# One fp32 decoder layer on a single core: the order of weight sums, of q's low parts, of a norm's steps and of attention's value products

## The chip, the cores and the metric

The kernel runs on one core of one Trainium2 chip. A core has a matrix engine (TensorE, in the profile PE, with its weight load as PEld), three engines for elementwise work (VectorE, DVE; ScalarE, ACT; GpSimd, POOL) and a queue engine (SyncE, SP) that here only issues transfers. SP, ACT and POOL issue transfers between DRAM and the core's own memory (SBUF); all of them take their instructions in order. The metric is the time of one execution on the device in microseconds (us).

## The reference

The layer takes x (512 tokens x 1024) and multiplies it with one weight matrix of 1024 x 9216. The columns are split into nine groups of 1024. Cut to what matters:

```python
h = x @ w_in
ua, va, za, qh, kh, vh, zb, ga, gb = split(h)
ua = gelu(ua)
va = layer_norm(gelu(va), a_ln_g, a_ln_b)
sa = einsum("gts,bnsgc->bntgc", tril(w_s), va in 4 chunks x 8 groups) + a_b_s
ya = ua * sa * silu(za)
q = rope(qh) * 64 ** -0.5            # 8 heads, two maps of 64 each
k = rope(kh)
o = diff_attention(q, k, vh, lam)    # softmax 1 - lam * softmax 2, causal, times v
yb = rms_norm(o) * g * silu(zb)
m = sigmoid(ga) * (ya @ w_branch_a) + sigmoid(gb) * (yb @ w_branch_b)
out = layer_norm(alpha * x + m @ w_out + sigmoid(x @ w_pg) * (p @ w_ple))
```

## The kernel before

Every fp32 product is made of three matmuls of the faster fp32r type: each operand is cut into a high part and a low part (for a weight: ACT copies `wh`, line 334; DVE subtracts to `wl`, line 337), and high x high, low x high and high x low are added in PSUM. One such matmul, 128x128 by 128x512, is called a product here.

PE works through stages one after another: k, q (pair 0), zb (pair 0), v, attention with the groups of k, q and zb of the next pair of heads between its small matmuls, ua, za, va, ga, gb, pg, the per-layer embedding, the two branch projections wb and wa, and the output. v, va, ga, gb, pg, wb and wa use a Strassen-like scheme, `quad`: seven steps of 24 products in place of eight, on quarters of the 1024x1024 weight and sums of them. In line with that, a weight quad has 14 half quarters or sums to be split.

There are two ways to those sums of weights. In a `quad` plan, POOL adds the next quarter onto the one in SBUF with an accumulating transfer (`follow`, line 308), as soon as DVE has read the old one for its low part; tiles that hold sums are called `wa`, others `wr`, three buffers each. In a `ready_quad` plan (before: only wb), four sums of two halves each lie in DRAM (`wsd`); they are made there during attention by `make_sums`: SP copies a quarter (a "begin", line 281), later POOL adds another onto it (an "add", line 279), and SP loads them afterwards like any weight (line 301).

The order of all this is written out by hand. `later(n, fn)` puts a step behind the n-th product from now, and tables of such numbers set where each step is issued: `TURN_Q` and the stack numbers for q's rotary step of pair 0 (multiplications on DVE, a join on POOL at lines 660 and 661, high halves `hl` on ACT at 666, low halves on POOL at 671, then the stacks: SP copies `q<-hl`, line 687), `ROPE` for later pairs, `VALUES` for the products of attention weights with v (line 771; `at` is their copy from the transposes, line 762), `TAIL` for a head's norm behind its values, `NORM` for va's layer norm (mean and factor on DVE and POOL, centring at line 1069, shift at 1073, statistics at 1065), `MAKE` for the sums in DRAM, `SPLITS` for a quad's `wh` and `wl`. On ACT the quads' intermediate sums `s` are copied from PSUM (line 563). For v, DVE and ACT also cut sums of x into parts, `piece` (line 865).

Of the kernel before, what the change touches and what calls it, by code (L numbers as in the profile page):

```python
# [39 lines left out]
HIGH = (2,)  # L40
LOW = (12,)
ROPE = (2, 6, 8, 14, 18)
STACK = (14, 4)
FIRST_STACK = (20, 4)
SWAP = 132
# [2 lines left out]
PERIOD = (13, 16, 20, 23)  # L48
COMBINE = (10, 10, 13, 11)
TURN = (23, 24, 32, 27)  # L50
VALUES = (34, 36, 41, 41)
TAIL = (2, 14, 26, 44)
NORM = (4, 50, 148, 172)
SPLITS = {"wb": ((4, 7), (13, 16)), "": ((1, 4), (8, 12))}
BEHIND = (8, 14)
GELU = 22
SILU = (20,)
SPATIAL = (222, 22)
MAKE = (2, 26, 146, 170, 290, 314, 440, 490)
TABLES = (30, 44)  # L60
TURN_K = (16, 19, 22, 25, 29, 36, 40)
TURN_Q = (28, 31, 36, 40, 46, 84, 88)
LAMBDAS = (130, 250, 324, 332)
FIRST_GATE = 168
SUMS_OF_X = (60, 66, 84, 90, 150, 158, 174, 182)
SUMS_OF_Y = (90, 120, 150, 180, 250, 268, 286, 304)
XS = (2, 2, 50, 14)
EARLY = 0
HELD = 2
CUT_YB = (2, 6)  # L70
# [30 lines left out]
def token_units(off):  # L101
    return [("t", off + c * T, kk) for c in range(2) for kk in range(4)]
# [16 lines left out]
def plan():  # L119

    units, steps, made_of = [], [], {}

    def add(name, w, us):
        for u in us:
            steps.append((name, len(units), "", None))  # L130
            units.append((w, u))

    def quad(name, w, us):
        first, last = len(units), {}
        units.extend((w, u) for u in us)
        for chain, quarter in CHAINS:
            for j in range(2):
                steps.append((name, first + QUARTERS[quarter][j], chain, last.get((chain, j))))
                last[chain, j] = len(steps) - 1

    def ready_quad(name, w, us):
        first = len(units)
        units.extend((w, u) for u in us)
        for what in READY:
            for j in range(2):
                unit = ("sum", what, j) if isinstance(what, int) else first + QUARTERS[what][j]
                steps.append((name, unit, "xy"[j], None))
        for q, us in QUARTERS.items():
            made_of[q] = [first + u for u in us]

    cols = [c for _, u in rope_units(KO, 0) + rope_units(QO, 0) for c in u]
    add("kq", "in", [("c", cols, kk) for kk in range(4)])
    add("zb", "in", feature_units(ZB, 2))
    add("ua", "in", feature_units(UA, EARLY))
    quad("v", "in", token_units(VO))
    for p in range(1, 4):
        add("k", "in", rope_units(KO, p))
        add("q", "in", rope_units(QO, p))
        add("zb", "in", feature_units(ZB + 2 * p * P, 2))
    add("ua", "in", feature_units(UA + EARLY * P, KT - EARLY))  # L160
    add("za", "in", feature_units(ZA, 8))
    quad("va", "in", token_units(VA))
    quad("ga", "in", token_units(GA))
    quad("gb", "in", token_units(GB))
    quad("pg", "pg", token_units(0))
    add("ple", "ple", [("p", 1), ("p", 0)])
    ready_quad("wb", "b", token_units(0))
    add("wa", "a", token_units(0))
    add("out", "out", token_units(0))
    return units, steps, made_of  # L170
# [33 lines left out]
def hybrid_layer(ctx: ExitStack, tc: tile.TileContext, a, out: bass.AP):  # L204
# [61 lines left out]


    sums = []
    wsd = dram.tile([4, 2, P, 1024], F32, name="wsd")

    def weights(unit):
        return W[unit] if isinstance(unit, int) else wsd[unit[1], unit[2]]

    def make_sums(at):

        def step(n, what, of, j):
            source = weights(("sum", of, j) if isinstance(of, int) else MADE_OF[of][j])
            if what == "add":
                pool.dma_start(out=wsd[n, j], in_=source, accum_op=OP.add, max_dma_last_dim=4096)
            else:  # L280
                sp.dma_start(out=wsd[n, j], in_=source)

        for i, (n, what, of) in enumerate(MAKING):
            for j in range(2):
                later(at[i] + 12 * j, step, n, what, of, j)

    def load(u, pieces=1, first=sp):
        if u >= len(STEPS) or u in raw or STEPS[u][3] is not None:
# [65 lines left out]
    def next_pair(name, i):  # L354
        u = cursor[0]
        assert STEPS[u][0] == name, (STEPS[u][0], name)
        cursor[0] += 2
        for j in range(4):
            assert u + j in raw, (u, j)
        run(prep(u))  # L360
        run(prep(u + 1))

        def ask(at, v, fits=lambda chain: True):
            if v < len(STEPS) and fits(STEPS[v][2]):
                later(at, lambda: run(load(v)))


        for v in range(u + 4, u + 8):
            ask(1, v, lambda chain: chain in ("x", "y"))
        within = [bool(v < len(STEPS) and STEPS[v][2]) for v in range(u, u + 6)]  # L370
        ask(1 if within[2] else 20, u + 6)
        ask(9, u + 5, lambda chain: chain != "b" and chain != "c")
        ask(12, u + 7, lambda chain: chain != "a" and (chain or within[4]))
        for j, at in enumerate(SPLITS.get(name, SPLITS[""])):

            spread(u + 2 + j, *(BEHIND if i == 5 and j and name != "wb" else at))
        return split.pop(u), split.pop(u + 1)

    def run(gen):
# [269 lines left out]

    def rope(name, p, banks=None, at=None, stack=STACK):  # L650

        A, B = banks or (pp(), pp())
        m, parts = [], []

        def turn(bank, table):
            m.append(ap_.tile([P, T], F32, name="m", tag="m", bufs=6))
            dve.tensor_tensor(out=m[-1], in0=bank, in1=table, op=OP.mult)

        def join():
            pool.tensor_tensor(out=m[0], in0=m[0], in1=m[3], op=OP.subtract)  # L660
            pool.tensor_tensor(out=m[2], in0=m[2], in1=m[1], op=OP.add)

        def high():
            parts.append(ap_.tile([P, 4, T], F32R, name="hl", tag="hl"))
            for j in range(2):
                act.activation(parts[0][:, j, :], m[2 * j], AF.Copy)

        def low():
            hl = parts[0]
            for j in range(2):  # L670
                pool.tensor_tensor(out=hl[:, 3 - j, :], in0=m[2 * j], in1=hl[:, j, :].bitcast(F32),
                                   op=OP.subtract)
            for hd in range(2):
                later(stack[0] + stack[1] * hd, get, hd)

        def get(hd):


            h = 2 * p + hd
            for n in ("k", "kx") if name == "k" and p else (name,):  # L680
                s = ap_.tile([P, 2, T], F32R, name=n, tag=n, bufs=3)
                stacks[n, h] = s
                for i in range(2):
                    rows = parts[0][2 * hd + i:P:4]
                    if n == "kx":
                        rows = rows[:, ::-1]
                    sp.dma_start(out=s[:, i, :].bitcast(F32), in_=rows.bitcast(F32))
            if name == "k" and p == 0:
                later(SWAP + 6 * hd, change_over, h)

        def change_over(h):
            s = ap_.tile([P, 2, T], F32R, name="kx", tag="kx", bufs=3)
            stacks["kx", h] = s
            for b in range(4):
                sp.dma_start(out=s[b:P:4].bitcast(F32), in_=stacks["k", h][3 - b:P:4].bitcast(F32))

        at = at or ROPE[:2] + ROPE
        for i, bank in enumerate((A, B)):
            if not banks:
                feature_group(bank, name, xh, xl)  # L700
            later(at[2 * i], turn, bank, cs)
            later(at[2 * i + 1], turn, bank, sn)
        for n, fn in zip(at[4:], (join, high, low)):
            later(n, fn)
# [186 lines left out]
            s = slice((k % 2) * T + i * P, (k % 2) * T + (i + 1) * P)  # L891
            three(bank, h[:, s], l[:, s], xh[:, k, :], xl[:, k, :], k == 0, k == KT - 1)
    rope("k", 0, first_kq[:2], TURN_K, FIRST_STACK)
    rope("q", 0, first_kq[2:], TURN_Q, FIRST_STACK)
    gate_b(0, (pbank("tr", 1), pbank("po", 1)), FIRST_GATE)

    ua = big.tile([P, KT, T], F32, name="ua", tag="U")
# [31 lines left out]
    quad("v", operands(xh, xl, [of_piece(j) for j in range(4)]),  # L929
         ([pp(), pp()], [pbank("sc", 2) for _ in range(2)], [pp(), pbank("tx", 1)]), place_v, v_done)  # L930
    sums.clear()
    make_sums(MAKE)
    for p in range(1, 4):
        attention(p - 1, BEGIN)
        rope("k", p)
# [125 lines left out]
    def va_norm(t):  # L1061
        st = small([P, 2, 6], "vst", 4)
        z = va[:, t, :]
        for c in range(2):
            dve.bn_stats(out=st[:, c, :], in_=va[:, t, c * T:(c + 1) * T])
        mv, rs = rstd_of(st)

        def centre():
            dve.scalar_tensor_tensor(out=z, in0=z, scalar=mv[:, 0:1], in1=ga_t,
                                     op0=OP.subtract, op1=OP.mult)  # L1070

        def shift():
            dve.scalar_tensor_tensor(out=z, in0=z, scalar=rs[:, 0:1], in1=ba_t,
                                     op0=OP.mult, op1=OP.add)

        later(8, centre)
        later(16, shift)

    def spatial(g):
        sa = pbank("tr" if g % 2 else "po", 1)  # L1080
# [233 lines left out]
```

## Time and profile before

| | us |
|---|---|
| three runs | 630.01, 630.9, 635.1 |
| their median | 630.9 |
| the profiled execution | 631.16 |
| its span on the core | 629.5 |
| PE's first product (k and q) | 5.27 |
| zb | 27.96 |
| v | 38.84 |
| attention | 79.95 |
| ua | 215.2 |
| za | 274.7 |
| va | 318.70 |
| ga | 358.40 |
| gb | 396.51 |
| pg | 441.4 |
| per-layer embedding | 481.3 |
| wb | 492.15 |
| wa | 530.2 |
| output | 575.6 |

The profile is of one execution, taken by the hardware; the rows of stages are the start of their first product. An engine's share of the span is the time in which an instruction of it ran. A row of the timeline has the start, the duration, the engine, the line, the operation with its output and inputs, the count of instructions in the row, and in brackets how long the engine was idle before it and what ended that. The granted clock is that of PE as a share of full speed.

### The profile page before, as it was taken

What the parts mean: (1) busy time and instruction counts of PE and PEld (TensorE: products, weight loads), DVE (VectorE), ACT (ScalarE), POOL (GpSimd) and SP (SyncE); (2) the same over time, 40 slices, a digit from 0 to 9 for tenths busy, and PEclk for the clock granted to TensorE, in tenths of its full rate; (3) what the DMA queues carried; (4) which work ended last, traced back from release to release, by engine and by line L of the source; (5) the groups of instructions that cost most, each with busy time, mean ns of one, the idle gap of its engine ahead of it and who ended that gap; (6) DMA issues with size and microseconds to landing.
All of it is one profiled execution on the core that took longest, in us unless ns stands there. A gap on an engine that the chain in (4) does not pass through costs nothing.

```text
span 629.5 us, 8313 instructions
## 1 busy us (share of the span) xinstructions
PE 615.2 (98%) x2929; PEld 509.7 (81%) x2929; DVE 452.1 (72%) x767; ACT 314.4 (50%) x510; POOL 131.2 (21%) x132
## 2 busy tenths in 40 slices
PE   8999999999999999999999999999999999999994
PEld 5887788888888888888887888788888888888884
DVE  5898667878878866844874796868757758676386
ACT  5544575554654655565464765445556446232200
POOL 2174003714424320220012131321120000000011
PEclk9999999999999999999999999999999999999998
DMA  8678895575555525436869779898997954865102
GB/s 301 205 201 203 222 325 203 157 179 199 202 134 201 204 74 141 154 131 218 281 176 254 190 192 215 247 206 247 244 215 275 399 185 155 287 209 185 34 35 100
DMA packets 45210, 125.66 MB, mean 200 GB/s; under 512 B 5744, under 2 KB 6576, under 8 KB 45040
## 3 DMA queue, kind: packets, MB, share of 16 engines
q1 hardware_dynamic: 35232, 95.04, 42.7%
q0 software_dynamic: 7200, 25.50, 21.7%
q10 hardware_dynamic: 2736, 4.59, 1.9%
q8 instruction: 23, 0.38, 0.2%
q14 instruction: 19, 0.16, 0.1%
HBM read 101.91 MB, written 19.01 MB: 192 GB/s over the span
## 4 chain that ended last, share of the span: by engine, by line
PE 69%; DMA 13%; issue 6%; DVE 6%; ACT 4%; POOL 2%; SPq 0%; ACTq 0%; DVEq 0%; POOLq 0%
PE ps_pp L238 39%; PE ps_sc L238 11%; DMA wa<-in_w 7%; PE ps_tx L238 5%; PE ps_sc L726 3%; DMA wr<-in_w 3%; PE ps_po L771 3%; DVE wl L337 3%; PE ps_tr L238 2%; PE ps_po L238 2%; ACT wh L334 2%; DMA xt<-in_xT 2%; PE ps_tr L760 1%; DMA xr<-in_xT 1%; PE ps_tr L1082 1%
## 5 line engine op out<-in xcount | busy, mean ns | idle before, releaser
L337 DVE TENSOR_TENSOR wl<-wr,wh 128x1024 fp32r<-128x1024 f32 x90 | 115.0, 1283 | 37.7 <-ACT wh L334 37.5
L334 ACT ACTIVATE wh<-wr 128x1024 fp32r<-128x1024 f32 x90 | 94.0, 1053 | 73.5 <-DMA wr<-in_w 28.5
L238 PE MATMUL ps_pp<-xh,wh 128*128 128x512 f32 x296 | 119.3, 403 | 0.6 <-ACT wh L264 0.6
L238 PE MATMUL ps_pp<-xh,wl 128*128 128x512 f32 x296 | 117.1, 396 | 0.1
L238 PE MATMUL ps_pp<-xl,wh 128*128 128x512 f32 x296 | 117.1, 396 | 0.0
L337 DVE TENSOR_TENSOR wl<-wa,wh 128x1024 fp32r<-128x1024 f32 x46 | 55.7, 1222 | 29.4 <-ACT wh L334 29.3
L238 PEld LDWEIGHTS ps_pp<-xh,wl 128*128 128x128 f32 x296 | 55.7, 188 | 11.3 <-DVE wl L265 0.4
L238 PEld LDWEIGHTS ps_pp<-xh,wh 128*128 128x128 f32 x296 | 55.8, 188 | 10.5 <-ACT wh L264 1.1
L238 PEld LDWEIGHTS ps_pp<-xl,wh 128*128 128x128 f32 x296 | 55.7, 188 | 10.3 <-DVE xl L265 0.2
L739 ACT ACTIVATE p<-p,sth 128x128 f32<-128x128 f32 (+3 forms) x64 | 35.5, 556 | 50.5 <-DVE sth L737 50.4
L334 ACT ACTIVATE wh<-wa 128x1024 fp32r<-128x1024 f32 x46 | 48.0, 1054 | 22.5 <-DMA wa<-in_w 16.9
L308 POOL DMA_DIRECT2D wa<-in_w x30 | 26.1, 869 | 129.6 <-DVE wl L337 93.5
L1055 POOL TENSOR_TENSOR rs<-mv,mhalf 128x1 f32<-128x1 f32 x8 | 10.5, 1312 | 174.2 <-DVE mv L1053 174.2
L733 DVE CUSTOM_DVE_ANT_0 p<-ps_sc,mask 128x128 f32<-128x128 f32 (+3 forms) x64 | 31.0, 484 | 11.8 <-PE ps_sc L726 11.7
L238 PE MATMUL ps_pp<-wl,xh 128*128 128x512 f32 x80 | 31.3, 391 | 1.0 <-DVE wl L337 1.0
L238 PE MATMUL ps_pp<-wh,xh 128*128 128x512 f32 x80 | 31.2, 390 | 0.0
L238 PE MATMUL ps_sc<-wl,xsh 128*128 128x512 f32 x80 | 31.2, 390 | 0.0
L238 PE MATMUL ps_sc<-wh,xsh 128*128 128x512 f32 x80 | 31.2, 390 | 0.0
L238 PE MATMUL ps_pp<-wh,xl 128*128 128x512 f32 x80 | 31.2, 390 | 0.0
L238 PE MATMUL ps_sc<-wh,xsl 128*128 128x512 f32 x80 | 31.1, 389 | 0.0
L797 POOL TENSOR_TENSOR f<-ss,mhalf 128x4 f32<-128x4 f32 x8 | 9.0, 1123 | 81.8 <-DVE ss L796 60.0
L771 PEld LDWEIGHTS ps_po<-v,at 128*128 128x128 f32 x160 | 22.5, 190 | 3.7 <-ACT at L762 1.3
(340 smaller groups left out, 1371.4 us busy)
## 6 DMA issues: line engine op xcount, KB each, us to landing
wr<-in_w SPq DMA_DIRECT2D x78, 512.0 KB, 4.2
wa<-in_w POOLq DMA_DIRECT2D x30, 512.0 KB, 7.9
wa<-in_w SPq DMA_DIRECT2D x13, 512.0 KB, 4.7
wr<-in_w POOLq DMA_DIRECT2D x10, 512.0 KB, 8.6
k<-hl SPq DMA_DIRECT2D x16, 256.0 KB, 2.5
q<-hl SPq DMA_DIRECT2D x16, 256.0 KB, 2.5
wsd<-in_w POOLq DMA_DIRECT2D x8, 512.0 KB, 7.7
kx<-hl SPq DMA_DIRECT2D x12, 256.0 KB, 2.6
```

The costliest lines, as they stand in the source:

```text
L238: pe.matmul(ps, s, m, start=start, stop=stop, skip_group_check=read_within)
L308: pool.dma_start(out=raw[u], in_=W[STEPS[FOLLOWS[u]][1]], accum_op=OP.add)
L334: act.activation(h, raw[u], AF.Copy)
L337: dve.tensor_tensor(out=l, in0=raw[u], in1=h.bitcast(F32), op=OP.subtract)
L726: pe.matmul(sc[m][:, :n], q[:, m, i * P:(i + 1) * P], kk[:, m, :n], start=o == 0, stop=o == 1)
L733: dve.tensor_tensor_reduce(out=pr[m][:, :n], in0=sc[m][:, :n], in1=mask[:, T - n:], scale=-(DK ** -0.5), scalar=3e38, op0=OP.add, op1=OP.m ...
L739: act.activation(pr[m][:, :n], pr[m][:, :n], AF.Exp, bias=st[:, m:m + 1], scale=-1.0, accum_out=st[:, 2 + m:3 + m])
L760: pe.transpose(tr[:, j * P:(j + 1) * P], ad[:, j * P:(j + 1) * P], ident)
L771: pe.matmul(po[:, i * P:(i + 1) * P], at[:, j * P:(j + 1) * P], v[:, j, h * P:(h + 1) * P], start=j == 0, stop=j == i)
L797: pool.tensor_tensor(out=f, in0=ss, in1=mhalf[:, :NT], op=OP.pow)
L1055: pool.tensor_tensor(out=rs, in0=mv[:, 1:2], in1=mhalf[:, 0:1], op=OP.pow)
L1082: pe.matmul(sa[:, t * P:(t + 1) * P], va[:, t, g * P:(g + 1) * P], wsT[:, g, :], start=True, stop=True)
```

## The change

First, va takes its sums from DRAM as wb does: `ready_quad` in place of `quad`. `make_sums` is called for both, with a DRAM tensor each (`ws_va`, `ws_wb`); va's steps take nearly the places that wb's had, and wb's go in between and behind, to product 530 and 12 more. Second, q of pair 0 gets its high and low halves at 140 and 146 instead of 84 and 88, with stacks 14 and 18 behind instead of 20 and 24; in later pairs the two halves come four products later. Third, va's centring and shift stand 12 and 20 products behind the mean instead of 8 and 16, and the four chunks' norms start at 4, 52, 156 and 184 instead of 4, 50, 148 and 172. Fourth, values stand one to three products of the table further on, and with the last of them a head's tail. What is computed stays the same.

```diff
+ROPE_Q = (2, 6, 8, 18, 22)
-VALUES = (34, 36, 41, 41)
+VALUES = (35, 37, 44, 43)
-NORM = (4, 50, 148, 172)
-SPLITS = {"wb": ((4, 7), (13, 16)), "": ((1, 4), (8, 12))}
+NORM = (4, 52, 156, 184)
+SPLITS = {"va": ((4, 7), (13, 16)), "wb": ((4, 7), (13, 16)), "": ((1, 4), (8, 12))}
+CENTRE = (12, 20)
-MAKE = (2, 26, 146, 170, 290, 314, 440, 490)
+READY_MADE = {'va': (2, 6, 26, 32, 146, 174, 290, 314), 'wb': (150, 290, 170, 318, 440, 464, 500, 530)}
+APART = 12
-TURN_Q = (28, 31, 36, 40, 46, 84, 88)
+TURN_Q = (28, 31, 36, 40, 46, 140, 146)
-XS = (2, 2, 50, 14)
+XS = (2, 2, 54, 14)
...
-    quad("va", "in", token_units(VA))
+    ready_quad("va", "in", token_units(VA))
...
-    wsd = dram.tile([4, 2, P, 1024], F32, name="wsd")
+    wsd = {n: dram.tile([4, 2, P, 1024], F32, name="ws_" + n) for n in READY_MADE}
...
-            spread(u + 2 + j, *(BEHIND if i == 5 and j and name != "wb" else at))
+            spread(u + 2 + j, *(BEHIND if i == 5 and j and name not in SPLITS else at))
...
-        at = at or ROPE[:2] + ROPE
+        at = at or ROPE[:2] + (ROPE if name == "k" else ROPE_Q)
...
-    rope("q", 0, first_kq[2:], TURN_Q, FIRST_STACK)
+    rope("q", 0, first_kq[2:], TURN_Q, STACK)
...
-    make_sums(MAKE)
+    for name, at in READY_MADE.items():
+        make_sums(name, at)
...
-        later(8, centre)
-        later(16, shift)
+        later(CENTRE[0], centre)
+        later(CENTRE[1], shift)
```

On POOL, from k's low halves of pair 0 through v to the first pair of attention, this stood before (`m` and `hl` are the rotary step's tiles, the loads into `wa` and `wr` are v's accumulates):

```order
L671 TENSOR_TENSOR hl<-m,hl 128x512 x2
L660 TENSOR_TENSOR m<-m 128x512
L661 TENSOR_TENSOR m<-m 128x512
L308 DMA wa<-in_w 128x1024 x2
L671 TENSOR_TENSOR hl<-m,hl 128x512 x2
L308 DMA wr<-in_w 128x1024 x2
L308 DMA wa<-in_w 128x1024 x2
L660 TENSOR_TENSOR m<-m 128x512
L661 TENSOR_TENSOR m<-m 128x512
L671 TENSOR_TENSOR hl<-m,hl 128x512 x2
```

On the same engine at the same place stands after the change:

```order
L676 TENSOR_TENSOR hl<-m,hl 128x512 x2
L665 TENSOR_TENSOR m<-m 128x512
L666 TENSOR_TENSOR m<-m 128x512
L313 DMA wa<-in_w 128x1024 x2
L313 DMA wr<-in_w 128x1024 x2
L313 DMA wa<-in_w 128x1024 x2
L676 TENSOR_TENSOR hl<-m,hl 128x512 x2
L284 DMA ws_va<-in_w 128x1024 x4
L665 TENSOR_TENSOR m<-m 128x512
L666 TENSOR_TENSOR m<-m 128x512
L676 TENSOR_TENSOR hl<-m,hl 128x512 x2
```

q's low halves moved behind all of v's accumulates, and four adds of va's sums now stand ahead of the first pair's join.

On DVE, at the passage from ga to gb (the `va` rows are a chunk's centring and shift, `vst` its statistics), the order before was this:

```order
L337 TENSOR_TENSOR wl<-wa,wh 128x1024 x2
L1069 SCALAR_TENSOR_TENSOR va<-va,mv,ga_t 128x1024
L1073 SCALAR_TENSOR_TENSOR va<-va,rs,ba_t 128x1024
L1065 BN_STATS vst<-va 128x6 x2
L1052 BN_AGGR mv<-vst 128x2
L1053 TENSOR_SCALAR mv<-mv 128x1
L337 TENSOR_TENSOR wl<-wr,wh 128x1024 x2
L1069 SCALAR_TENSOR_TENSOR va<-va,mv,ga_t 128x1024
L1073 SCALAR_TENSOR_TENSOR va<-va,rs,ba_t 128x1024
```

After the change the same passage on DVE reads:

```order
L342 TENSOR_TENSOR wl<-wa,wh 128x1024
L1075 SCALAR_TENSOR_TENSOR va<-va,mv,ga_t 128x1024
L342 TENSOR_TENSOR wl<-wr,wh 128x1024
L1079 SCALAR_TENSOR_TENSOR va<-va,rs,ba_t 128x1024
L342 TENSOR_TENSOR wl<-wr,wh 128x1024
L1071 BN_STATS vst<-va 128x6 x2
L1058 BN_AGGR mv<-vst 128x2
L1059 TENSOR_SCALAR mv<-mv 128x1
L1075 SCALAR_TENSOR_TENSOR va<-va,mv,ga_t 128x1024
```

Each of gb's first two low parts `wl<-wr` moved ahead: one stands behind the centring alone, the other behind the shift, and the statistics come after both.

On POOL, from the last head's norm to the norm of va, eight accumulates stood before:

```order
L804 TENSOR_TENSOR on<-on,f 128x512
L308 DMA wa<-in_w 128x1024 x4
L308 DMA wr<-in_w 128x1024 x2
L308 DMA wa<-in_w 128x1024 x2
L1040 AFFINE_SELECT aux<-aux 128x1024
L308 DMA wa<-in_w 128x1024 x2
```

After the change this stands there:

```order
L803 TENSOR_TENSOR f<-f,ok 128x4
L809 TENSOR_TENSOR on<-on,f 128x512
L1046 AFFINE_SELECT aux<-aux 128x1024
L313 DMA wa<-in_w 128x1024 x2
L1061 TENSOR_TENSOR rs<-mv,mhalf 128x1
```

va's accumulates are gone; the first ones that follow are ga's.

More of the change, by code (lines that the diff above doesn't have):

```diff
@@ L145, in ready_quad @@
             for j in range(2):
-                unit = ("sum", what, j) if isinstance(what, int) else first + QUARTERS[what][j]
+                unit = (name, what, j) if isinstance(what, int) else first + QUARTERS[what][j]
                 steps.append((name, unit, "xy"[j], None))
         for q, us in QUARTERS.items():
-            made_of[q] = [first + u for u in us]
+            made_of[name, q] = [first + u for u in us]
     cols = [c for _, u in rope_units(KO, 0) + rope_units(QO, 0) for c in u]
@@ L268, in hybrid_layer, with make_sums @@
     sums = []
-    wsd = dram.tile([4, 2, P, 1024], F32, name="wsd")
+    wsd = {n: dram.tile([4, 2, P, 1024], F32, name="ws_" + n) for n in READY_MADE}
     def weights(unit):
-        return W[unit] if isinstance(unit, int) else wsd[unit[1], unit[2]]
-    def make_sums(at):
+        return W[unit] if isinstance(unit, int) else wsd[unit[0]][unit[1], unit[2]]
+    def make_sums(name, at):
+        there = wsd[name]
         def step(n, what, of, j):
-            source = weights(("sum", of, j) if isinstance(of, int) else MADE_OF[of][j])
+            source = weights((name, of, j) if isinstance(of, int) else MADE_OF[name, of][j])
             if what == "add":
-                pool.dma_start(out=wsd[n, j], in_=source, accum_op=OP.add, max_dma_last_dim=4096)
+                pool.dma_start(out=there[n, j], in_=source, accum_op=OP.add, max_dma_last_dim=4096)
             else:
-                sp.dma_start(out=wsd[n, j], in_=source)
+                sp.dma_start(out=there[n, j], in_=source)
         for i, (n, what, of) in enumerate(MAKING):
             for j in range(2):
-                later(at[i] + 12 * j, step, n, what, of, j)
+                later(at[i] + APART * j, step, n, what, of, j)
     def load(u, pieces=1, first=sp):
```

## The prediction

> **What bounds the kernel now.** I read the page's busy times first, then PE's table of waits, then a table of stages, and only then the timeline at the places where PE stops.
>
> ```profile
> span 629.5 us, 8313 instructions
> PE 615.2 (98%) x2929; PEld 509.7 (81%) x2929; DVE 452.1 (72%) x767; ACT 314.4 (50%) x510; POOL 131.2 (21%) x132
> PE ps_pp L238 <- DVE wl L337: 2.7, 3, 1.0
> PEld ps_po L771 <- ACT at L762: 1.3, 3, 0.5
> ```
>
> PE is busy for 98% of the span, so only its stops can be won. The waits (idle us, times, longest) name a few: three times a low part `wl`, three times the attention weights `at`. The stages tell what each stop costs. The columns are window, length, PE, PEld, DVE, ACT and POOL busy (instructions), granted clock, DMA share, GB/s; the rows are the quads of v, va, ga and wb, 168 products each.
>
> ```profile
> 38.84:79.95 41.11, 38.66 (x169) 31.38 (x168) 31.40 (x34) 22.21 (x29) 14.63 (x12) 1.00 0.86 216
> 318.70:358.40 39.70, 38.93 (x170) 31.38 (x168) 23.74 (x26) 23.38 (x30) 7.63 (x9) 1.00 0.84 219
> 358.40:396.51 38.11, 38.11 (x170) 31.51 (x169) 28.02 (x34) 22.42 (x28) 9.98 (x11) 1.00 0.88 213
> 492.15:530.23 38.08, 38.08 (x170) 31.53 (x169) 25.29 (x32) 20.46 (x26) 0.00 (x0) 1.00 0.67 243
> ```
>
> The same work takes 38.08 in wb, whose sums lie ready in DRAM, 0.227 a product. Against that v loses 41.11 - 38.08 = 3.03 and va 1.62, at full clock. Two smaller losses, behind values and at the start of gb, come below.
>
> **The change, part by part.** *q's parts in v.* Here is v's chain.
>
> ```profile
> 29.88 1.47 DVE L865 TENSOR_TENSOR piece<-raw,piece 128x512 fp32r<-128x512 f32 x2
> 50.64 2.87 POOL L671 TENSOR_TENSOR hl<-m,hl 128x512 fp32r<-128x512 f32 x2
> 50.90 3.77 DVE L865 TENSOR_TENSOR piece<-raw,piece 128x512 fp32r<-128x512 f32 x2
> 56.45 0.50 PE L238 MATMUL ps_pp<-wl,xsy 128*128 128x512 f32 x1 [0.91 <-DVE wl L337]
> 56.70 0.87 POOL L308 DMA_DIRECT2D wr<-in_w  x1 [3.19 <-DVE wl L337]
> 60.11 0.86 POOL L308 DMA_DIRECT2D wa<-in_w  x1 [0.29 <-DVE wl L337]
> 64.86 1.06 ACT L334 ACTIVATE wh<-wr 128x1024 fp32r<-128x1024 f32 x1 [6.34 <-DMA wr<-in_w]
> 65.95 1.23 DVE L337 TENSOR_TENSOR wl<-wr,wh 128x1024 fp32r<-128x1024 f32 x1 [6.15 <-ACT wh L334]
> 68.31 1.07 ACT L563 ACTIVATE s<-ps_sc 128x512 f32<-128x512 f32 x2
> 68.94 0.50 PE L238 MATMUL ps_sc<-wh,piece 128*128 128x512 f32 x1 [1.54 <-ACT s L563]
> 73.01 1.06 ACT L334 ACTIVATE wh<-wa 128x1024 fp32r<-128x1024 f32 x1 [2.09 <-DMA wa<-in_w]
> 83.13 0.22 PE L726 MATMUL ps_sc<-k,q 128*128 128x128 f32 x1
> ```
>
> POOL subtracts q's low parts while DVE makes two low pieces, which take 3.77 instead of 1.47. The low part behind them comes late, PE waits 0.91, POOL can issue its accumulating load only at 56.70, that lands for ACT at 64.86, and the copies `s`, queued behind on ACT, keep PE until 68.94. The change moves these subtractions, their high halves, two stacks and four SP copies 52 to 58 products on, of 0.227: POOL's from 50.64 to some 62.5 us, the SP copies to 66. POOL has then issued v's last accumulate (60.11), and DVE was idle 6.15 before 65.95, so nothing due waits on either there. ACT gets two half copies behind `wh<-wa`; SP issues the q copies behind two weight loads. The first scores, at 83.13, leave them over 10 us.
>
> I win 2.3 of the 3.03: the 2.30 by which the pieces were stretched. The bounds are 0 (the transfers set the landing anyway, as the 2.09 before 73.01 warns) and 3.03. The Trainium skill, in "SBUF — State Buffer", section "Who interferes with whom", has DVE with two SBUF inputs and GpSimd lock each other out for a whole instruction. By that rule the pieces lose up to POOL's whole 2.87, and this sum would be 2.9 in place of 2.3. The 3.77 against 1.47 bears out a lock, but shows 2.30 of it.
>
> *Values one to three products on.* Values now stand further behind the transposes whose copies they wait for.
>
> ```profile
> 118.86 0.39 PE L238 MATMUL ps_pp<-xh,wl 128*128 128x512 f32 x1
> 119.29 0.71 PE L771 MATMUL ps_po<-v,at 128*128 128x128 f32 x4
> ```
>
> A stop costs PE more than its idle time: a record lasts 0.39 where starts come 0.227 apart, which hides 0.16, and the first matmul behind a stop takes 0.50 (as at 56.45), 0.11 more. Here 119.29 - 118.86 - 0.227 = 0.20, with the 0.11 some 0.3, three times: 0.9. PE's weight load waits 1.3 / 3 = 0.43 for the copy `at`; the values of a head's fourth block now come two products, 0.45, later, which just covers it. I win 0.7 (bounds 0 and 0.9; 0 if a head's tail, whose steps move by two products as well, stops PE instead).
>
> *va's sums in DRAM.* va's first quarter waits for POOL's accumulating load.
>
> ```profile
> 328.57 0.87 POOL L308 DMA_DIRECT2D wa<-in_w  x1 [0.27 <-DVE wl L337]
> 340.76 1.06 ACT L334 ACTIVATE wh<-wa 128x1024 fp32r<-128x1024 f32 x1 [2.06 <-DMA wa<-in_w]
> 343.14 0.50 PE L238 MATMUL ps_pp<-wl,xsh 128*128 128x512 f32 x1 [0.76 <-DVE wl L337]
> ```
>
> It takes 340.76 - 328.57 = 12.2. va had six plain loads and eight accumulates; now it has 14 plain loads. Then va looks like wb: I win 1.5 of 1.62 (bounds 0, if a plain load comes as late, and 1.62). ACT and DVE do the same conversions; earlier split times `(4,7),(13,16)` are those wb runs with.
>
> *va's norm.* At gb's first products DVE was busy with centre, shift and statistics of rows that nobody waited for.
>
> ```profile
> 399.23 1.28 DVE L1073 SCALAR_TENSOR_TENSOR va<-va,rs,ba_t 128x1024 f32<-128x1024 f32 x1
> 402.10 2.36 DVE L337 TENSOR_TENSOR wl<-wr,wh 128x1024 fp32r<-128x1024 f32 x2
> 403.38 0.50 PE L238 MATMUL ps_pp<-wl,xh 128*128 128x512 f32 x1 [1.04 <-DVE wl L337]
> ```
>
> PE loses 1.04 + 0.16 + 0.11 = 1.3. Now only centre stands ahead of the first `wl`, which comes 2 x 1.28 or more earlier: 1.1 won (0 to 1.30). What is late next is the statistics behind it, used only by the spatial products in gb's later half.
>
> *What it adds.* Eight SP copies and eight POOL accumulates of 512 KB, in attention and ua. POOL needs 8 x 1.03 = 8 more there, and the transfers their share:
>
> ```profile
> q1 hardware_dynamic: 35232, 95.04, 42.7%
> q0 software_dynamic: 7200, 25.50, 21.7%
> 120.00:140.00 20.00, 20.00 (x108) 16.98 (x108) 14.40 (x43) 13.03 (x27) 5.28 (x7) 1.00 0.85 207
> 140.00:160.00 20.00, 20.00 (x109) 17.05 (x108) 17.23 (x37) 8.84 (x23) 10.83 (x9) 1.00 0.43 159
> L279 POOL DMA_DIRECT2D wsd<-in_w x8: 817/1031/1772, 121.7 to 236.0; - x8
> DMA to landing us min/median/max: 4.2/6.7/14.0
> ```
>
> q0's 25.50 MB are about 48 transfers of 0.52 MB: 0.217 x 629.5 / 48 = 2.85 us of all 16 engines each; q1's cost 0.427 x 629.5 / 181 = 1.48. So 16 transfers cost 35 to 46 us, over some 135 us of which nearly half was free (0.43 and 0.85 by turns). The nearest rows are 120 to 140 and ga's stage, which lose 0 and 0.03 at 0.85 and 0.88; the worst is v's, 3.03 of 41.11 or 7% at 0.86. If half of 135 us ran like v, that were 0.07 x 67 = 5. I take 0.3, by the nearest (bounds 0 and 5). In va 8 x (2.85 - 1.48) = 11 us of transfer go.
>
> Sum: 2.3 + 0.7 + 1.5 + 1.1 - 0.3 = 5.3. The profiled execution took 631.16, its span of 629.5 and 1.66 around it; 631.16 - 5.3 = 625.9. The runs' median, 630.9, lies 0.26 lower, so 625.6. The tail behind 600, where PE has stops of its own, isn't touched.
>
> **The rivals.**
>
> *All of it is won:* 3.03 + 0.9 + 1.62 + 1.3 = 6.8, so 624.1. For it, four separate places with plain causes; against it, v's landings are paced by the transfers.
>
> *The gain comes back at the next place that waits for transfers.* v at 0.86 and ga at 0.88 are as full as va was. If v only moves its stop to the last accumulate, 2.3 becomes 0.3, and if ga, which starts 1.5 earlier with its accumulates behind va's loads, gives back half of va's 1.5, 5.3 becomes 2.6: 628.3. The 2.09 before 73.01 speaks for it, ga's 38.11 without a stop against it.
>
> *The added transfers stop attention.* At 120 to 140 the share is 0.85 already; 16 more transfers at 2.85 leave weights late. Between 2 and the bound of 5 is 3.5 lost: 630.9 - 5.6 + 3.5 = 628.8. The Trainium skill, "DMA: Bandwidth & Descriptors", section "Issuing engines are not separate DMA queues", says that all issuers share the same 16 engines. That agrees with the shares above, which count both queues.
>
> *Slower: POOL stands before an accumulate.* An accumulate must wait for the copy it adds to, and POOL does its queue in order. In the first pair four of them now stand ahead of POOL's joins for k, behind which ACT has q's and k's high halves, exponentials and weights.
>
> ```profile
> 85.79 1.13 SPq L281 DMA_DIRECT2D wsd<-in_w  x2
> 94.30 1.28 POOL L660 TENSOR_TENSOR m<-m 128x512 f32<-128x512 f32 x1 [33.34 <-DVE r L747]
> 95.62 0.64 ACT L666 ACTIVATE hl<-m 128x512 fp32r<-128x512 f32 x1 [0.96 <-POOL m L660]
> 99.05 0.72 ACT L739 ACTIVATE p<-p,sth 128x512 f32<-128x512 f32 x1 [1.25 <-DVE sth L737]
> POOL wsd L279 <- DMA wsd<-wsd: 5.2, 1, 5.2
> ```
>
> The last copy is issued by 86.9; landing L later and with 1.03 for the add, POOL comes to `m` at 87.9 + L. Against 94.30, and with ACT's slack of 1.25, the delay is L - 7.6. At the median 6.7 it is nothing, at the longest 14.0 it is 6.4; it outweighs the 5.6 won from L = 13.2 on. At 14.0: 630.9 - 5.6 + 6.4 = 631.7, a hair slower. For it, such copies did take 14.0 once and POOL did wait 5.2; against it, half of such copies landed within 6.7.
>
> *Nothing happens:* every stop is taken over by another engine's lateness at the same place, 630.6.
>
> **How the numbers follow.** Forecast (624.5 to 627) 0.55; all won 0.08; given back 0.14; attention 0.12; POOL 0.06; nothing 0.05. The prediction is the forecast's 625.6. From 623.9 (all won) to 629.6 the range leaves out POOL, nothing, and a little at both ends, under 2 in 10. A change of 1%, 6.3 us, is about what a measurement here tells from none: faster than 624.6 needs nearly all won, 0.15; slower than 637.2 would need POOL's price twice, 0.03; within 0.82.
>
> **What would show it.** Of the changed kernel: the pieces in v near 1.5 a pair and its stage near 38.8; no wait of PE's weight load for `at`; va at 38.1 to 38.3 with no POOL load in it; gb without the stop. Wrong if v still stops near 69 for `s`, if POOL waits over 8 us for a copy in the first pair, or if PE is less than full between 80 and 275.

## The result, and the profile after the change

| | before | changed |
|---|---|---|
| median of seven runs, us | 632.62 | 627.33 |
| lowest to highest | 630.01 to 635.1 | 626.22 to 629.13 |
| span of the profiled execution | 629.5 | 625.2 |

The ratio is 0.992, with a 95% interval of 0.9893 to 0.9948: 5.3 us less. A later comparison of the same two kernels gave 0.9904 (0.9885 to 0.9924). The three runs known when the prediction was made had a median of 630.9; with the runs beside the changed kernel it is 632.62, so the 5.3 that were forecast as a difference were met more closely than the 625.6 as a time.

The page's first lines and PE's waits of the changed kernel, in the same columns as before:

```profile
span 625.2 us, 8346 instructions
PE 613.8 (98%) x2929; PEld 510.5 (82%) x2929; DVE 448.0 (72%) x767; ACT 313.8 (50%) x510; POOL 128.6 (21%) x132
PE ps_pp L241 <- ACT s L568: 1.0, 1, 1.0
PE ps_tr L765 <- DVE p L756: 0.6, 2, 0.3
PE ps_pp L241 <- DVE wl L342: 0.5, 1, 0.5
```

None of the waits that the prediction named is left. The copy `s` that stops PE now is one in ga, the low part one in gb, and the transposes (`ps_tr`) did not stop PE before. The stages, by the same table of windows (v, the first two pairs of attention, va, ga, gb):

```profile
38.53:76.61 38.08, 38.08 (x170) 31.54 (x168) 31.31 (x33) 22.44 (x29) 14.46 (x12) 1.00 0.93 241
76.61:119.12 42.51, 42.51 (x216) 35.79 (x215) 31.68 (x85) 23.34 (x53) 16.71 (x15) 1.00 0.85 264
119.12:165.40 46.28, 45.96 (x245) 38.84 (x244) 37.40 (x94) 25.34 (x57) 20.29 (x18) 1.00 0.75 226
315.16:353.24 38.08, 38.08 (x169) 31.54 (x168) 22.84 (x26) 23.11 (x30) 3.12 (x3) 1.00 0.61 207
353.24:392.60 39.36, 38.40 (x169) 31.46 (x168) 28.21 (x35) 21.58 (x28) 9.15 (x11) 1.00 0.88 209
392.60:437.14 44.54, 44.02 (x217) 36.75 (x216) 34.67 (x40) 22.87 (x30) 9.19 (x10) 1.00 0.92 225
```

v and va now take 38.08, exactly what wb takes: nothing of their losses is left. ga, which had none, has become 1.25 longer. The next table has the stages of every profiled execution of the study, each from the start of its first product (the 96th, 144th, 312th and so on of 2424) to the start of the next stage's. The stages left out differ by 0.06 at most; the first product comes at 5.13 to 5.75.

| kernel | k, q | v | pair 1 | pair 2 | pair 3 | va | ga | gb | span |
|---|---|---|---|---|---|---|---|---|---|
| before | 22.69 | 41.11 | 42.86 | 46.17 | 46.19 | 39.70 | 38.11 | 44.87 | 629.5 |
| changed | 22.39 | 38.08 | 42.51 | 46.28 | 46.29 | 38.08 | 39.36 | 44.54 | 625.2 |
| changed, again | 22.47 | 38.08 | 42.49 | 46.27 | 46.27 | 38.08 | 38.76 | 44.41 | 624.9 |
| e1: ga split early | 22.79 | 38.08 | 44.21 | 46.32 | 46.27 | 38.08 | 38.09 | 44.32 | 625.9 |
| e2: norm back | 22.60 | 38.08 | 44.50 | 46.39 | 46.29 | 38.08 | 38.51 | 44.91 | 626.9 |
| e3: values back | 22.87 | 38.08 | 46.27 | 45.75 | 45.75 | 38.08 | 38.36 | 43.52 | 626.3 |
| e4: q's halves early, stacks late | 22.52 | 39.39 | 42.39 | 46.34 | 46.32 | 38.08 | 38.21 | 44.43 | 625.4 |
| e5: before + q of pair 0 | 22.37 | 38.08 | 42.83 | 46.16 | 46.19 | 40.13 | 38.53 | 46.05 | 628.4 |
| e7: copies later | 24.18 | 38.08 | 42.39 | 46.31 | 46.27 | 38.08 | 38.49 | 43.52 | 625.5 |
| e8: before + values | 24.28 | 40.55 | 42.51 | 46.31 | 46.28 | 38.96 | 38.08 | 45.32 | 630.5 |
| e9: adds behind the join | 22.38 | 38.08 | 49.95 | 45.76 | 45.75 | 38.08 | 38.10 | 44.18 | 630.3 |
| e10: before + q of later pairs | 22.43 | 41.65 | 42.43 | 45.75 | 45.75 | 39.37 | 38.08 | 44.85 | 628.2 |
| e11: three edits | 22.39 | 38.08 | 42.59 | 45.75 | 45.75 | 38.08 | 38.08 | 43.87 | 622.7 |
| e11, again | 22.42 | 38.08 | 42.43 | 45.75 | 45.75 | 38.08 | 38.08 | 44.54 | 623.2 |

From before to the changed kernel the sum is: k and q -0.30, v -3.03, pair 1 -0.35, pairs 2 and 3 +0.21, ua -0.06, va -1.62, ga +1.25, gb -0.33, together -4.2 of the 4.3 by which the span fell. So there were gains of 5.7 and losses of 1.5. The 0.30 of k and q is no work of the change: e5 and e10, which leave that stage as before, took 22.37 and 22.43. The three pairs, whose stops at values were counted as 0.7 won, gave 0.14 together (0.35 won in pair 1, 0.21 lost in the other two).

### The profile page after: what moved, and what is told of

It is laid out like the page before. It is cut to its first block, busy times and chain, and to the rows that moved or that the text cites. A ratio compares the mean times of both kernels' runs of the same rounds, so it can differ in the third digit from the quotient of the medians.

```text
span 625.2 us, 8346 instructions
## 1 busy us (share of the span) xinstructions
PE 613.8 (98%) x2929; PEld 510.5 (82%) x2929; DVE 448.0 (72%) x767; ACT 313.8 (50%) x510; POOL 128.6 (21%) x132
## 4 chain that ended last, share of the span: by engine, by line
PE 86%; DMA 5%; issue 4%; DVE 3%; ACT 1%; POOL 0%; DVEq 0%; POOLq 0%; ACTq 0%
PE ps_pp L241 50%; PE ps_sc L241 14%; PE ps_tx L241 7%; PE ps_sc L731 3%; DMA wa<-in_w 3%; PE ps_tr L241 3%; PE ps_po L241 3%; PE ps_po L776 3%; DMA wr<-in_w 2%; PE ps_tr L765 1%; DVE wl L342 1%; ACT wh L339 1%; DMA xr<-in_xT 1%; PE ps_po L1088 1%; PE ps_tr L1088 1%
## 5 line engine op out<-in xcount | busy, mean ns | idle before, releaser
L342 DVE TENSOR_TENSOR wl<-wr,wh 128x1024 fp32r<-128x1024 f32 x91 | 116.6, 1286 | 31.6 <-ACT wh L339 28.9
L339 ACT ACTIVATE wh<-wr 128x1024 fp32r<-128x1024 f32 x91 | 95.2, 1053 | 69.2 <-DMA wr<-in_w 22.9
L339 ACT ACTIVATE wh<-wa 128x1024 fp32r<-128x1024 f32 x45 | 46.6, 1052 | 14.9 <-DMA wa<-in_w 7.8
L313 POOL DMA_DIRECT2D wa<-in_w x24 | 20.6, 859 | 105.1 <-DVE wl L342 104.9
L676 POOL TENSOR_TENSOR hl<-m,hl 128x512 fp32r<-128x512 f32 x16 | 22.9, 1488 | 5.3 <-ACT hl L671 5.3
```

The lines of the kernel that those rows point to most:

```text
L313: pool.dma_start(out=raw[u], in_=W[STEPS[FOLLOWS[u]][1]], accum_op=OP.add)
L339: act.activation(h, raw[u], AF.Copy)
L342: dve.tensor_tensor(out=l, in0=raw[u], in1=h.bitcast(F32), op=OP.subtract)
```

## The experiments

**e1, ga's first units split early.** In the changed kernel va's last step prepares ga's first weights by va's new split times. This run gives that step the old ones.

```diff
-        for j, at in enumerate(SPLITS.get(name, SPLITS[""])):
+        for j, at in enumerate(SPLITS.get("" if name == "va" and i == 6 else name, SPLITS[""])):
```

> The changed kernel with one thing undone: at va's last step the first two weight units of ga are split at (1,4) and (8,12) again, not at va's new (4,7) and (13,16). Theory A (the new stop of PE in ga, 1.12 + 0.11, comes because ga's first accumulates are issued 1 to 2 us later and accumulates land one behind the other): the stop in ga goes, the one at gb's first step (0.68 + 0.11), which is late by the same chain, goes or halves; span 625.2 - 1.2 to 2.0 = 623.2 to 624.0. Rival B (centre and shift or the norm's new places delay ga's low parts): both stops stay, 625.2. Rival C (ga's stop is a matter of transfers in general, because ga starts 5.9 us earlier): the stop stays within 0.3.

ga took 38.09: its stop went. gb's stayed, which theory A had seen as late by the same chain. And pair 1 took 44.21, 1.7 more than in the first profile, at a place that the edit doesn't touch. Here are ga's accumulates in the changed kernel (ga starts at 353.25):

```profile
351.86 0.94 POOL L313 DMA_DIRECT2D wa<-in_w  x1 [25.55 <-DVE wl L342]
353.00 0.84 POOL L313 DMA_DIRECT2D wa<-in_w  x1 [0.20 <-issue]
369.23 0.84 POOL L313 DMA_DIRECT2D wr<-in_w  x1 [0.18 <-issue]
379.97 1.06 ACT L339 ACTIVATE wh<-wr 128x1024 fp32r<-128x1024 f32 x1 [1.43 <-DMA wr<-in_w]
381.57 0.50 PE L241 MATMUL ps_pp<-wh,xsh 128*128 128x512 f32 x1 [0.96 <-ACT s L568]
```

And the same two places in e1 (ga starts at 355.42), the first accumulate and the last split:

```profile
352.30 0.94 POOL L313 DMA_DIRECT2D wa<-in_w  x1 [23.82 <-DVE wl L342]
380.83 1.06 ACT L339 ACTIVATE wh<-wr 128x1024 fp32r<-128x1024 f32 x1 [1.43 <-DMA wr<-in_w]
```

The first accumulate goes out 3.12 ahead of ga in e1, 1.39 ahead in the changed kernel. The second accumulate into `wr` is issued 15.98 behind ga's start in both, but it lands for ACT 25.41 behind it in e1 and 26.72 in the changed kernel. On ACT the copies `s` stand behind that split, and PE needs them. Over all executions ga's length follows this one number: up to 25.45 it is 38.08 to 38.11, at 25.56 it is 38.21, at 25.69 it is 38.36, at 25.90 it is 38.51, at 26.13 it is 38.76 and at 26.72 it is 39.36. So with the late split ga stands at the edge, and the landing decides how much it loses, from 0.1 to 1.25 in six executions. With the early split it lost nothing in four of four (e1, e9, e11 twice); among the four executions with va's plan as before, e5 lost 0.42 with a landing at 25.93, so an early split alone is no guarantee.

**e2, the norm's places back.**

```diff
-NORM = (4, 52, 156, 184)
+NORM = (4, 50, 148, 172)
-CENTRE = (12, 20)
+CENTRE = (8, 16)
```

> The changed kernel with NORM and CENTRE as before. Theory A (split times): ga's stop of 1.2 stays, and gb's old stop at its first low part from wr, 1.3, comes back on top or in place of the 0.8; span 625.2 to 626.5. Rival B (the norm's places cause ga's stop): ga's stop goes, span 624 to 625.3.

ga's stop was 0.41 here: smaller, but by the landing (25.90), as the row of numbers above shows, not by the norm. gb's old stop came back:

```profile
400.85 0.50 PE L241 MATMUL ps_pp<-wl,xh 128*128 128x512 f32 x1 [1.00 <-DVE wl L342]
```

So the norm's new places do what they were counted for. The new stop at gb's first step did not come in this execution.

**e3, values back.**

```diff
-VALUES = (35, 37, 44, 43)
+VALUES = (34, 36, 41, 41)
```

> The changed kernel with VALUES as before, and so with a head's tail as before. Theory (the tail moved with the last values, and its two elementwise steps on DVE now delay the combination before two transposes): the two stops of 0.49 at transposes go, three of 0.3 at values come back, so 625.2 within 0.2. Rival (the transposes wait because q's halves of later pairs moved on POOL): the transposes still stop, span 626.0.

Pairs 2 and 3 took 45.75, less than either kernel: the transposes no longer stop, and the values don't stop either, though they stand where they stood before. Neither theory had that. Pair 1 took 46.27, which is told below.

**e4, q's halves early, stacks late.**

```diff
-TURN_Q = (28, 31, 36, 40, 46, 140, 146)
+TURN_Q = (28, 31, 36, 40, 46, 84, 88)
...
-    rope("q", 0, first_kq[2:], TURN_Q, STACK)
+    rope("q", 0, first_kq[2:], TURN_Q, (72, 4))
```

> The changed kernel with q's halves of pair 0 at 84 and 88 again, but the stacks where the change put them. Theory (POOL's subtractions stretch DVE's pieces, and everything late in v follows from that): the pieces take 3.8 in place of 1.5 again and v loses about 3.0, span 628.2. Rival (the SP copies of the stacks hold up the accumulates' landing): the pieces may be stretched, but v loses under 1.3, span under 626.5.

v took 39.39, between 38.08 and 41.11. Its rows:

```profile
50.59 2.86 POOL L676 TENSOR_TENSOR hl<-m,hl 128x512 fp32r<-128x512 f32 x2
50.85 3.76 DVE L870 TENSOR_TENSOR piece<-raw,piece 128x512 fp32r<-128x512 f32 x2
56.40 0.50 PE L241 MATMUL ps_pp<-wl,xsy 128*128 128x512 f32 x1 [1.01 <-DVE wl L342]
56.64 0.86 POOL L313 DMA_DIRECT2D wr<-in_w  x1 [3.19 <-DVE wl L342]
62.04 1.06 ACT L339 ACTIVATE wh<-wr 128x1024 fp32r<-128x1024 f32 x1 [3.62 <-DMA wr<-in_w]
```

The pieces are stretched as before the change, PE stops at 56.40 as it did at 56.45, and POOL issues the accumulate at 56.64, as it did at 56.70. But it lands for ACT at 62.04, not at 64.86, and the second stop (68.94 before) is not there. What differs is that SP's four copies `q<-hl`, 1 MB that went out at 53.53 before the change, now go out at 64.81. So the two stops had two causes: the stretched pieces cost 39.39 - 38.08 = 1.31, and the stacks' copies, which went between the accumulates, the other 1.72. The sizes are those of one execution: with both causes left as before, v took 40.55 in e8 and 41.65 in e10.

**The changed kernel again**, with no edit.

> The changed kernel once more. Theory (POOL's first join after the four adds falls beside DVE's low part of the weights at some 92 us, and which of them comes first is decided by the landing of the copies): the first pair's stage takes either 42.4 to 42.6, with that low part at 1.2, or 44 to 46, with it over 6; ga 38.1 to 39.4. Rival (the stop belongs to the experiments' edits): 42.5 and 39.4 as in the first profile, within 0.1.

Pair 1 took 42.49 and ga 38.76. Pair 1 had been longer in e1, e2 and e3, none of which touches it before that point. The rows that tell it, first of the changed kernel, then of e3:

```profile
91.75 1.22 DVE L342 TENSOR_TENSOR wl<-wr,wh 128x1024 fp32r<-128x1024 f32 x1
93.01 1.58 POOL L665 TENSOR_TENSOR m<-m 128x512 f32<-128x512 f32 x1
```

```profile
92.07 1.58 POOL L665 TENSOR_TENSOR m<-m 128x512 f32<-128x512 f32 x1
92.11 6.35 DVE L342 TENSOR_TENSOR wl<-wr,wh 128x1024 fp32r<-128x1024 f32 x1
93.32 1.58 POOL L666 TENSOR_TENSOR m<-m 128x512 f32<-128x512 f32 x1
94.56 2.81 POOL L676 TENSOR_TENSOR hl<-m,hl 128x512 fp32r<-128x512 f32 x2
102.19 1.07 PE L776 MATMUL ps_po<-v,at 128*128 128x128 f32 x5 [1.99 <-ACT at L767]
```

When POOL's join begins about when DVE's subtraction does, that takes over 6 in place of 1.22: in all three such executions it ends 1.09 behind the last of POOL's four instructions (two of the join, two of the halves), as if it had only begun to run there. Everything of DVE's queue then comes 5 us later and PE stops. The subtraction began 15.14 or 15.15 behind the stage's start in every execution with the four adds there. The join began at 15.11, 15.12 and 15.44 in the three with the long form (6.35, 6.37, 6.67), and at 15.63 to 16.86 in the six with 1.22. So the subtraction lost even in e2, where by the rows it began 0.29 ahead of the join, and kept its time in e4, where it began 0.49 ahead. POOL comes to the join 0.54 behind its last add. That add waits for the landing of a copy. In e1 and e3 the copy had landed in time: the add went out at 14.57, and the profile names DVE's `rho` as what released it. From `rho` DVE comes to its subtraction at 15.14 by itself. So it is an early landing that makes the two meet, and a late one that keeps them apart. It cost 1.7, 2.0 and 3.8 in pair 1, in three of six executions of kernels with the change's own places for copies and adds. In e3 part of the 3.8 is the clock: behind a stop of 2 us PE's granted clock was 0.50 from 104 to 106 us. Before the change the join waited for DVE and began at 14.35, the subtraction at 15.97 behind it took 2.29. There DVE came in between two of POOL's instructions; why it does not in e3 the runs don't show.

**e5, before with q of pair 0 moved** (in the kernel before, `TURN_Q` ends with 140 and 146 and the stacks go by `STACK`; nothing else is changed).

> The kernel before with only q's halves and stacks of pair 0 moved. Theory: v's stage takes 38.1 in place of 41.11, everything else is as before, span 629.5 - 3.0 = 626.5. Rival (the gain is given back at the next place that waits for transfers): v gains under 2 or a later stage loses over 1; span over 627.5.

v took 38.08: the part alone wins all 3.03. But the span fell by 1.1 only. va, ga and gb were 0.43, 0.42 and 1.18 longer, each at a place that waits for the landing of a transfer (in ga, 25.93 behind the start by the number above). By its numbers this is the rival's case, but one execution can't say how much of that is due to the earlier start, and how much changes from one execution to the next.

**e7, copies later.**

```diff
-READY_MADE = {'va': (2, 6, 26, 32, 146, 174, 290, 314), ...
+READY_MADE = {'va': (14, 18, 26, 32, 146, 174, 290, 314), ...
```

> The changed kernel with the four copies that begin va's sums 12 products (about 3.9 us) later, the adds where they were. Theory on the lock (POOL's join then comes behind DVE's low part): that low part takes 1.2. Theory on the queue (POOL stands before an add, its join comes some 3.9 later, ACT stands at q's and k's high halves and the exponentials behind them are late): ACT waits over 5 for POOL and the first pair's stage takes 44 to 46. Rival (there is slack): 42.5 within 0.3.

Pair 1 took 42.39 and the low part 1.22. But POOL's join came only at 16.58 behind the stage's start, against 16.40 and 15.96 in the changed kernel: the copies were behind weight loads on SP anyhow. That agrees with the theory on the lock, but one execution can't show that the later copies prevent the meeting, as half of the executions without them had none either. What a join 4 us later would cost was not tried. The longer k and q stage is ten products at the start that came 0.43 apart in place of 0.227.

**e9, adds behind the join**, with e1's and e3's edits:

```diff
-READY_MADE = {'va': (2, 6, 26, 32, 146, 174, 290, 314), ...
+READY_MADE = {'va': (2, 6, 72, 78, 146, 174, 290, 314), ...
```

> The changed kernel with three edits: the first four adds of va's sums at 72 and 78 (behind the first pair's join for k) in place of 26 and 32, VALUES as before, and ga's first two units split early as in the first experiment. By the theories: first pair 42.3 to 42.9 with no low part over 2.5 us, second and third pair 45.75 each in place of 46.28, ga 38.1; span 625.2 - 0.5 - 0.5 - 1.25 = 622.9 (622.0 to 623.6), and against the kernel before 1.0 to 1.2% less. Rival (values or transposes stop again, or ga's accumulates are late for another reason): span 624.5 or more.

The ratio was 0.9995 (0.9982 to 1.0008): all that the change brings was gone, in one place. Pair 1 took 49.95.

```profile
97.43 3.37 POOL L284 DMA_DIRECT2D ws_va<-in_w  x4
100.49 1.25 SPq L692 DMA_DIRECT2D k<-hl  x2
117.43 1.15 ACT L671 ACTIVATE hl<-m 128x512 fp32r<-128x512 f32 x2 [6.73 <-DMA wr<-in_w]
DMA to landing us min/median/max: 2.0/2.6/15.3
```

The last row is of the tile `hl`. The four adds now go out together, between SP's copies of k's stacks (`k` and `kx`), and all eight of these took 6.5 to 15.3 to land, where the median over the execution is 2.6 and the longest in the changed kernel 7.2. `hl` has a single buffer, so ACT can't write q's halves into it until k's copies have read it. The row's releaser is named as a weight load, which that instruction doesn't read; the copies are the transfers on which it can wait. ACT's weights `at`, behind `hl` in its queue, then stopped PE for 5.04 at 121.04, and the products behind that stop came 0.43 apart at a granted clock of 0.50 (123 to 125.5 us), which is most of the rest of the 7.4. The low part was no longer met by POOL's join at this cost (2.30, as before the change), ga took 38.10, and pairs 2 and 3 took 45.75.

**e11, three edits together**: e7's places for the copies, e3's and e1's edits.

> The changed kernel with three edits, each tried singly before: the copies that begin va's sums at 14 and 18 (adds where the change has them), VALUES as before, ga's first two units split early. Theory: first pair 42.4, second and third 45.75 each, ga 38.1, gb 43.5 to 44.5; span 622 to 622.9, and by time 1.3 to 1.6% under the kernel before (ratio 0.984 to 0.988). Rival (the three don't add up, since each moves what the next stage waits for): ratio 0.990 or more, as for the changed kernel.

The stages came out as expected, with a span of 622.7, but the ratio was 0.9915 (0.9889 to 0.9941). So it was run once more.

> The kernel of the run before with three edits, once more, since its profiled execution (span 622.7) and its median did not fit. Theory (POOL's join and DVE's low part still meet in some executions, at a cost of 2 to 4 each): ratio 0.988 to 0.992, and if this profile holds such a meeting, the low part takes over 6 and the first pair 44 to 46. Rival (the first profile was typical and the medians were off): ratio under 0.988, first pair 42.5, span under 623.

0.9901 (0.9882 to 0.992), span 623.2, no meeting of join and low part (the join at 15.82). Two profiled spans of 622.7 and 623.2 against 625.2 and 624.9 say some 2 us less than the changed kernel; the ratios of 0.9915 and 0.9901 against 0.992 and 0.9904 don't tell the two apart. Whether the timed executions hold meetings that the two profiles didn't stays open.

**e8, before with VALUES alone.**

> The kernel before with only VALUES changed. Theory (the later values carry the head's tail with them): the three stops at values of 0.3 go, two stops at transposes of about 0.5 come, second and third pair 46.1 to 46.4 each; span within 0.4 of before. Rival (it is q's later halves that stop the transposes): no stop at transposes, second and third pair 45.8, span 0.9 less.

Pairs 2 and 3 took 46.31 and 46.28: the stops at values went, and two at transposes came in their place (0.35 and 0.31). That is the theory. Pair 1, where no stop at a transpose came, won 0.35. The span was 1.0 above the one before, not within 0.4 of it, since k and q took 1.6 more.

**e10, before with q's halves of later pairs four products later** (`ROPE_Q` alone).

> The kernel before with only q's halves of the later pairs four products later. Theory (that alone takes POOL's subtraction off the combinations behind which the values waited): the stops at values go, second and third pair 45.75 each, span 0.9 to 1.2 less than before. Rival (the stops at values stay until VALUES moves): 46.2 each, span as before.

45.75 each, and no stop at values or transposes. So this small part of the change, which the prediction gave no price, wins 0.43, 0.42 and 0.44 in the three pairs, 1.29 together: all of the values' stops, which were estimated at 0.9. VALUES isn't needed for it, and in the changed kernel the later values take the gain of pairs 2 and 3 away again. The mechanism is read from the timelines, first of the changed kernel, then of e10 at the same place:

```profile
203.61 2.71 POOL L676 TENSOR_TENSOR hl<-m,hl 128x512 fp32r<-128x512 f32 x2 [1.77 <-ACT hl L671]
203.68 1.51 DVE L756 SCALAR_TENSOR_TENSOR p<-p,rho,p 128x256 f32<-128x256 f32 x1
205.24 0.44 PE L765 MATMUL ps_tr<-ident,p 128*128 128x128 f32 x2 [0.32 <-DVE p L756]
207.61 1.02 POOL L802 TENSOR_TENSOR f<-ss,mhalf 128x4 f32<-128x4 f32 x1 [1.28 <-DVE r L752]
```

```profile
206.43 0.49 DVE L752 SCALAR_TENSOR_TENSOR p<-p,rho,p 128x256 f32<-128x256 f32 x1
209.35 1.02 POOL L798 TENSOR_TENSOR f<-ss,mhalf 128x4 f32<-128x4 f32 x1 [4.75 <-DVE r L748]
211.45 2.54 POOL L672 TENSOR_TENSOR hl<-m,hl 128x512 fp32r<-128x512 f32 x2
```

The combination `p` takes 1.51 beside POOL's subtraction of q's low halves and 0.49 without it. In the kernel before the two stood side by side too (1.50), and what came late there were the values. In e10 the later halves fall behind `f`, a step of the head's tail, in POOL's queue, and `f` waits for DVE, so the subtraction comes some 5 us later and `p` is free of it. With the last values the tail comes two products later, `f` is behind the halves again, and the subtraction is back beside `p`. And `p`, which stands behind the tail on DVE, begins 0.4 later in its stage than before, so now the transposes come late.

## Why the prediction was right, point by point

- *q's parts in v, 2.3 won:* the term was too small; it measured 3.03, and e5 shows that this part alone wins it. The step that failed is the chain from the pieces to the landing: "POOL can issue its accumulating load only at 56.70, that lands for ACT at 64.86". e4 issued it at the same time and it landed 2.8 earlier. The stretch of the pieces is worth 1.31, and the stacks' copies, mentioned only as something that moves, 1.72. The upper bound was reached.
- *Values, 0.7 won:* 0.14 came. The case that the prediction named with a bound of 0, that the head's tail stops PE instead, is what happened in pairs 2 and 3. e8 and e3 show it from both sides, and e10 shows that q's later halves alone win 1.29 at these stops.
- *va's sums, 1.5 won:* right, 1.62, in all executions with it. No run tells the plain loads from the new split times. The prediction calls these times, (4,7) and (13,16), earlier; they are 3 to 5 products later than (1,4) and (8,12), which cost nothing in va and did in ga.
- *va's norm, 1.1 won:* the old stop is gone, and e2 brings it back (1.16 by starts). But gb as a whole won 0.33. A weight load that lands 0.1 ahead of gb's start, not 0.9 ahead as before, now stops its eighth product by 0.7:

```profile
386.27 0.33 SPq L306 DMA_DIRECT2D wa<-in_w  x1
392.50 1.06 ACT L339 ACTIVATE wh<-wa 128x1024 fp32r<-128x1024 f32 x1 [3.26 <-DMA wa<-in_w]
394.88 0.50 PE L241 MATMUL ps_pp<-wl,xh 128*128 128x512 f32 x1 [0.52 <-DVE wl L342]
```

  In e3 and e7 it landed 1.1 and 1.4 ahead and gb took 43.52, which is the full gain. What sets that landing stays open. It is not the norm's places alone, since with the old ones it came anywhere from 0.95 ahead (e10) to 0.30 behind (e5).
- *What it adds, 0.3 lost in attention:* no loss in pair 1 in three of the six executions with the change's own places, and 1.7 to 3.8 in the three others. The step that was missing is the passage of POOL's join to the time of DVE's low part. The slower rival had the place right (POOL's adds ahead of the first join), but its price was a queue's; in the profile POOL was 2 us later than before against the stage's start and ACT's wait cost PE nothing. The lock did. The transfers themselves cost pairs 2 and 3 nothing: 45.75 with them (e3, e11) and without them (e10). PE is less than full there in the changed kernel, a sign that the prediction named, but by the values' 0.32 at the transposes, twice.
- *The gain comes back at the next place that waits for transfers:* held as a minor case: ga gave back 0.1 to 1.25, but by an earlier cause than ga's start, the split times at the seam from va to ga. That `SPLITS` of va also moves ga's first units was not counted.
- *The sum:* 5.3 was forecast; the medians gave 5.3 and, in the second comparison, 6.3, the two profiles 4.3. That the first of these meets the forecast is in part luck. By the profiles v brought 0.7 too much, the 0.3 for attention was not lost, and 0.4 came in k, q, ua and 0.1 in va; against that the pairs brought 0.6 too little, gb 0.8 too little, and ga lost 1.25 that the sum did not have. Why the medians lie further apart than the two profiled executions stays open.

On the lock the Trainium skill ("SBUF — State Buffer", section "Who interferes with whom") says of such a conflict that issue order decides which of the two blocks, and that whoever is first has the shared ports for its whole instruction. The rows agree in e1 and e3, where the join began first and DVE waited, and in e4, where DVE began 0.49 ahead, kept its 1.22, and the join took 1.88 in place of 1.58. They don't agree in e2, where by the starts on record DVE was 0.29 ahead and still waited. And they show more than one instruction's length: in e3 the 6.35 spans all four POOL instructions (rows of 1.58, 1.58 and 2.81), through which DVE did not come in.

## What to carry to other kernels

An instruction that only fills an idle engine is not free if it shares a resource with one that is on time: look at what stands beside it on the other engine, at both ends of the range in which it can start, above all where its start hangs on a transfer's landing. When a table of times is given to a stage, check the seam: its last steps prepare the next stage. And a loss that shows at a later stop of a chain may have a cause of its own; undo the parts one by one before the chain is believed.

## What the runs showed of the hardware

- A DVE subtraction with two inputs in SBUF took 6.35 to 6.67 in place of 1.22 when four POOL instructions that read SBUF began between 0.04 ahead of it and 0.29 behind it, and 1.22 when they began 0.49 or more behind it.
- In e9 four accumulating transfers that went out together held up the plain copies issued among and behind them: 6.5 to 15.3 to land against a median of 2.6.
- Behind a stop of PE of 5.04 (e9) or 1.99 (e3) the granted clock was 0.50 for a while, and products came 0.43 apart in place of 0.227.
- The executions differ at the start: the k and q stage took 22.4 to 22.9 in most and 24.2 and 24.3 in two (e7, e8), where the first ten or eleven products came 0.43 apart, against two to four of the first in the others.
